# Where the first norm's token rows are loaded and who makes the convolution's small copies, in a decoder layer on one NeuronCore

## The chip, the core and the metric

The kernel runs on one core of one Trainium2 chip. A core has five engines that work side by side, each on its own list of instructions, in order: TensorE (PE in the profile; its weight loads are shown apart as PEld), VectorE (DVE), ScalarE (ACT), GpSimd (POOL) and SyncE (SP), which here issues the DMA transfers. They wait for each other by semaphores. The metric is device time in microseconds (us) of one execution. Lower is better.

## What is computed

One decoder layer over 2048 tokens of 1024 channels, in float32: a norm, one input projection whose columns feed two token mixers (an S5 state space group and an RG-LRU group), an output projection with residual, a second norm with a SwiGLU network, and a last norm. The part that matters here:

```python
h = rms_norm(x, norm1_g[l])
proj = h @ w_in[l]
u = proj[..., :W_S5]
xr = proj[..., W_S5:W_S5 + W_LRU]
yr = proj[..., W_S5 + W_LRU:]
...
xpad = jnp.pad(xf, ((0, 0), (CONV_WIDTH - 1, 0), (0, 0)))
conv = conv_b.astype(f32) + sum(xpad[:, k:k + seq, :] * cw[k] for k in range(CONV_WIDTH))
```

and `rms_norm` multiplies each token's row by 1/sqrt(mean(x^2) + eps) and a gain for each channel.

## The kernel before

The tokens are cut into four blocks of 512 (TB). Data is held with channels on the 128 partitions and the tokens of a block along the free dimension, so the input projection of a block is twelve products, each of 8 chunks of 128 input channels. A float32 operand is split into a high and a low part, and each chunk takes three matmuls (high by high, high by low, low by high): 24 matmuls for one product. Each weight unit is loaded in two parts of 256 KB (`wraw`), cast to its high part on ACT (`whi`), and its low part is a subtraction on DVE or POOL (`wlo`); block 0 stores the low parts for the other blocks (`wlc`).

The norm's factor is not applied to x. The products are made from x times the gain, and each product's result is multiplied by the factor of its token on its way out of PSUM (`rs`, 128 x 512, the same row on all partitions). That is done by `evac_u`, `conv` and `gate_y`. The factor comes from a second copy of the same tokens with the tokens on the partitions (`xn`, four loads of 128 tokens x 1024 channels, 512 KB each): `stat_load` loads one, `stat` squares it on ACT and adds up its columns in the same instruction, `rsqrt` makes the inverse root on DVE in thirteen small steps, and `SumSq.spread` spreads it by TensorE to all partitions and copies it out on ACT. Until `rs` is there, no product leaves PSUM. The products have two banks `acc`, and the third and fourth product of block 0 go to two further ones, `y`.

The convolution (`conv`, four times in a block) puts a product, times the factor, into `xr` behind the last four columns of the block before, which are kept in `halo`; L660 on ACT makes the first tap, three instructions L663 on DVE the others.

Meanwhile the S5 tables are built once, by long runs of small instructions on DVE and POOL (`s5_build`, `s5_table`, `s5_w`, `s5_cp`). `s5_build` is held back on DVE until the first norm's inverse root has been made (`tc.issue_after(last["rs"])`, L560).

The order is a plan: `at(t, fn)` puts a piece of work at a time t of a written schedule (in units of its own, negative ones for what precedes the first product), the pieces are run through in order of t, and a scheduler then orders each engine's list by that priority and by when it reckons that operands are ready. The finished lists are fixed. Tiles come from pools: a tile of one tag with `bufs=1` is filled again only when its last reader is done. `xq` is such a tile; `rT` with `bufs=2` in the code of the change is two tags, `r` and `T`, with two tiles each of 128 x 2 x 512, first used by the gates of block 0 (L675) and by `decay`.

SP issues nearly all transfers, in order. In the plan the first ones are the first half of the first weights (-18.0), x in four loads of 512 KB (-17.9, -17.0, -15.0, -14.9), the second half (-15.4), the first token rows (-13.0), then the following weights (from -12.8), the other token rows behind (-10.5, -8.0, -5.5), and `eye` at -1.0, which `SumSq.spread` needs.

Of the kernel before, what the change touches and what calls it, by code (L numbers as in the profile page):

```python
# [13 lines left out]
ALU = mybir.AluOpType  # L14
# [3 lines left out]
SEQ, DM, TB = 2048, 1024, 512  # L18
# [4 lines left out]
CT = 8  # L23
NC = SEQ // CT
CB = TB // CT
# [34 lines left out]
class Plan:  # L60
# [3 lines left out]
    def at(self, t, fn):  # L64
        self.ev.append((t, len(self.ev), fn))
# [14 lines left out]
def build(tc, nc, I, O, ctx):  # L80
    pl = Plan()
    at = pl.at
    PE, DV, AC, GP, SP = nc.tensor, nc.vector, nc.scalar, nc.gpsimd, nc.sync
# [6 lines left out]
    eye = P.tile([128, 128], F32, name="eye")  # L90
    sA, sQ = ExitStack(), ExitStack()
    A = sA.enter_context(tc.tile_pool(name="A", bufs=1, side="right", reuse_waits="tile"))
    Q = sQ.enter_context(tc.tile_pool(name="Q", bufs=1, reuse_waits="tile"))
# [20 lines left out]
    halo = P.tile([128, 4, 4], F32, name="halo")  # L114
    h0 = P.tile([128, 4], F32, name="h0")
# [18 lines left out]
    xT, out = I["xT"], O  # L134

    def pc(name, i=None, n=1):
        if name in MCOLS:
            a, b = MCOLS[name]
            return pmat[:, a:b]
        a, b = PCOLS[name]  # L140
        return par[:, a:b] if i is None else par[:, a + i:a + i + n]
# [6 lines left out]
    def act(**kw):  # L148

        ins = AC.activation(**kw)  # L150
        ins = getattr(ins, "ins", ins)
        if "i" in last:
            tc.add_manual_dep(ins, last["i"].name, NOSYNC, reason="tables")
        last["i"] = ins

    def aux(tag, bufs=1):
        return PS.tile([128, TB], F32, tag=tag, name=tag, bufs=bufs)
# [7 lines left out]
    def r_(ap):  # L165
        return ap.bitcast(R)
# [54 lines left out]
    def rsqrt(ss, n, room):  # L221

        w_ = ss.shape[-1]
        mp, y, b = (room[:, (i + 1) * w_:(i + 2) * w_] for i in range(3))
        v = P.tile([128, 3, w_], F32, tag=f"nv{w_}", name="nv", bufs=2)
        ms, w, r = v[:, 0, :], v[:, 1, :], v[:, 2, :]
        DV.tensor_scalar(out=mp, in0=ss, scalar1=1.0 / n, scalar2=EPS, op0=ALU.mult, op1=ALU.add)

        DV.tensor_scalar(out=b.bitcast(I32), in0=mp.bitcast(I32), scalar1=1, scalar2=None, op0=ALU.logical_shift_right)
        DV.tensor_copy(out=ms, in_=mp)  # L230
        DV.tensor_scalar(out=y.bitcast(I32), in0=b.bitcast(I32), scalar1=-1.0, scalar2=float(0x5F3759DF),
                         op0=ALU.mult, op1=ALU.add)
        for i in range(3):
            DV.scalar_tensor_tensor(out=w, in0=y, scalar=-0.5, in1=ms, op0=ALU.mult, op1=ALU.mult)
            DV.tensor_tensor(out=w, in0=w, in1=y, op=ALU.mult)
            ins = DV.scalar_tensor_tensor(out=r if i == 2 else y, in0=w, scalar=1.5, in1=y, op0=ALU.add, op1=ALU.mult)
        last.setdefault("rs", getattr(ins, "ins", ins))
        return r
# [69 lines left out]
    pL = sL.enter_context(tc.tile_pool(name="L", bufs=1, reuse_waits="tile"))  # L308
    pW = sW.enter_context(tc.tile_pool(name="W", bufs=1, side="right", reuse_waits="tile"))
    pmat = pW.tile([128, NMAT], F32, name="pmat")  # L310
    at(-1.0, lambda: SP.dma_start(eye, I["eye"]))
    at(4.0, lambda: SP.dma_start(pmat, I["pmat"]))


# [25 lines left out]
    def s5_build():  # L340
        def sm(name, shape=(128, NQ, 16)):
            return pW.tile(list(shape), F32, name=name)
# [5 lines left out]
        em, h, x2, kk, p = (sm(n) for n in ("em", "h", "x2", "kk", "p"))  # L348
# [40 lines left out]
        nr, ni, s, a, c, cr, ci = (sm(n, (128, NQ)) for n in ("nr", "ni", "ss", "aa", "cc", "cr", "ci"))  # L389
# [25 lines left out]
        Q, Qd = (t.rearrange("p a b -> p (a b)").rearrange("p (r q j) -> p r q j", r=2, q=NQ) for t in (mag, em))  # L415
# [5 lines left out]
        TT(out=tq, in0=Pi[:, :, 0:8], in1=crb, op=ALU.mult)  # L421
        TT(out=Q[:, 1], in0=Q[:, 1], in1=tq, op=ALU.add)
        for t in range(CT):
            DV.tensor_copy(out=Qd[:, :, :, t], in_=Q[:, :, :, CT - 1 - t])

        N = [cm[:, :, 0:CT + 1], h[:, :, 0:CT + 1]]
        TS(out=N[0], in0=Pr[:, :, 0:CT + 1], scalar1=-1.0, scalar2=None, op0=ALU.mult)
# [131 lines left out]
    def s5_start():  # L559
        with tc.issue_after(last["rs"]):  # L560
            s5_build()
# [23 lines left out]
    def lt(tag, shape=(128, 2, TB), dt=F32, bufs=1):  # L585
        return pL.tile(list(shape), dt, tag=tag, name=tag, bufs=bufs)
# [19 lines left out]
    def nat(ap):  # L606
        return ap.rearrange("p (t c) -> p c t", t=CT)

    def seq(ap):
        return ap.rearrange("p (c t) -> p c t", t=CT)  # L610

    def in_tb(b, t0):
        H, L = actH, actL
        cur = {}
        sl = SumSq(4, "sumg", 2)
        tx, dx = (t0 - 6.5, 0.5) if b == 0 else (t0 - 5.0, 0.6)
        ts = t0 - 4.0 if b == 0 else t0 - 58.0
# [11 lines left out]


        def stat_load(i):
            cur["q", i] = lt("xq", (128, DM), bufs=1)
            SP.dma_start(cur["q", i], I["xn"][b * TB + 128 * i:b * TB + 128 * i + 128, :])

        def stat(i):
            if i == 0:
                cur["ss"] = P.tile([128, 4], F32, tag="ssq", name="ssq", bufs=2)
            q = cur.pop(("q", i))
            AC.activation(out=q, in_=q, func=AF.Square, accum_out=cur["ss"][:, i:i + 1])

        for i in range(4):
            at(ts + 2.5 * i - (9.0 if b == 0 else 5.0), lambda i=i: stat_load(i))
            at(ts + 2.5 * i, lambda i=i: stat(i))
        at(ts + 9.0, lambda: cur.__setitem__("rs", SumSq.spread(rsqrt(cur["ss"], DM, aux("nm")))))

        def evac_u(m):
            us = v_us[:, m % 2, :]
# [5 lines left out]
        def conv(m):  # L653
            h, i = divmod(m, 2)
            xr, xh = v_xr[i], v_xh[h]
            DV.tensor_copy(out=xr[:, 0:4], in_=halo[:, m, :])
            DV.tensor_tensor(out=seq(xr[:, 4:TB + 4]), in0=nat(cur.pop(("ps", 4 + m))), in1=nat(cur["rs"]),
                             op=ALU.mult)
            DV.tensor_copy(out=halo[:, m, :], in_=xr[:, TB:TB + 4])
            AC.activation(out=xh[:, i, :], in_=xr[:, 4:TB + 4], func=AF.Identity,  # L660
                          bias=pc("cb", m), scale=pc("cw", 12 + m))
            for k in (2, 1, 0):
                DV.scalar_tensor_tensor(out=xh[:, i, :], in0=xr[:, 1 + k:1 + k + TB],  # L663
                                        scalar=pc("cw", 4 * k + m), in1=xh[:, i, :],
                                        op0=ALU.mult, op1=ALU.add)
            if i == 1:
                AC.copy(r_(v_hh), xh)
                GP.tensor_tensor(out=r_(v_hl), in0=xh, in1=v_hh, op=ALU.subtract)
# [23 lines left out]
        def scan():  # L692
            for h in range(2):
                a, q = cur["r", h], cur["T", h]

                DV.scalar_tensor_tensor(out=a, in0=a, scalar=1.0, in1=q, op0=ALU.add, op1=ALU.mult)
                AC.activation(out=a, in_=a, func=AF.Identity, scale=-1.0, bias=1.0)
                act(out=q, in_=q, func=AF.Sqrt)
                DV.scalar_tensor_tensor(out=q, in0=a, scalar=1.0, in1=q, op0=ALU.add, op1=ALU.mult)
                DV.tensor_tensor(out=q, in0=q, in1=v_xh[h], op=ALU.mult)  # L700
                for i in range(2):
                    m = 2 * h + i
                    DV.tensor_tensor_scan(out=q[:, i, :], data0=a[:, i, :], data1=q[:, i, :],
                                          initial=h0[:, m:m + 1], op0=ALU.mult, op1=ALU.add)
                    DV.tensor_copy(out=h0[:, m:m + 1], in_=q[:, i, TB - 1:TB])

        def gate_y(m):
            h, i = divmod(m, 2)
# [18 lines left out]
        t = t0  # L727
        for i, m in enumerate((4, 5, 6, 7, 0, 1, 2, 3, 8, 9, 10, 11)):
            u = Unit(t, I["w_in"][m], 8, GP if i % 3 == 2 else DV, *((wlc[m], None) if b == 0 else (None, wlc[m])))

            def prod(m=m, u=u, i=i):
                cur["ps", m] = aux("y", 2) if b == 0 and i in (2, 3) else acc()
                mm3(cur["ps", m], u, [(k, k) for k in range(8)], chunks_of(H), chunks_of(L), True, True)

            at(t, prod)
            t += 8 * PT
            if m < 4:
                at(t + 0.5, lambda m=m: evac_u(m))
            elif m < 8:
                at(t + 0.5, lambda m=m: conv(m - 4))  # L740
            else:
                at(t + 0.5, lambda m=m: gate_y(m - 8))
            if i == 3:
                at(t + 0.2, lambda: gates(0))
                t += 2.6
            if i == 5:
                at(t + 0.2, lambda: gates(1))
                t += 2.6
                at(t + 2, decay)
                at(t + 2 + 3, scan)  # L750
            if i in (9, 11):
                at(t + 1.0, lambda h=i // 11: lru_out(h))
# [4 lines left out]
    for b in range(NB):  # L757
        tin.append(T)
        T = in_tb(b, T)
# [800 lines left out]
```

## Time and profile before

| what | us |
|---|---|
| three runs, median (lowest to highest) | 2141.07 (2137.44 to 2143.06) |
| the profiled execution's own time | 2144.24 |
| its span, first to last instruction | 2142.5 |
| input projection, S5 tables and LRU of all blocks, about | 0 to 460 |

How to read the lines that follow. A line of the timeline has the start, the time taken, the engine, the line of the kernel, the operation, what it writes and reads, the count, and in brackets how long the engine had been idle and what ended that. A line of the groups has the count, busy time in all, mean in ns of one, and the idle time in front of the group with what ended it. A line of the waits says who waited for whom: us in all, times, longest. SPq is SP's list of transfers; its durations are those of issuing one, not of the transfer. A table by stage has the stretch, its length, busy time and count for each engine, the clock granted to TensorE, the DMA engines' share and their rate.

### The profile page before, as it was taken

The numbers are of one execution on the slowest core, as the hardware profiler recorded it, in microseconds if no ns is written. First come the engines' busy times: TensorE is split into PE (matmuls) and PEld (weight loads), VectorE is DVE, ScalarE is ACT, GpSimd is POOL, SyncE is SP. The second block draws the span as 40 slices with busy tenths as digits, with TensorE's granted clock in tenths as the row PEclk, the third lists the DMA queues.
The fourth block names the chain that finished last, engine by engine and source line by source line (L and its number), as shares of the span: only waits on it lengthen the run. The fifth ranks groups of instructions, "written<-read, shape, count | busy, mean of one in ns | idle before, by whom it ended". The sixth has DMA issues, their size and how long they took to land.

```text
span 2142.5 us, 26006 instructions
## 1 busy us (share of the span) xinstructions
PE 1949.6 (91%) x8600; PEld 1556.4 (73%) x8600; DVE 1220.4 (57%) x1927; ACT 797.4 (37%) x1308; POOL 1012.7 (47%) x836
## 2 busy tenths in 40 slices
PE   6849999887989987999999989999999999999996
PEld 4637777765767766777777767777777888888785
DVE  5997578478547676544444554444434436654644
ACT  4634654463253242223223442322322343333331
POOL 1576246458734458655455543123123237544542
PEclk8968999988999989999999999999999999999998
DMA  8656998875644788644444564444443578754733
GB/s 292 203 171 194 270 298 260 225 191 158 201 128 144 245 273 298 213 149 156 148 146 159 192 206 148 127 139 147 126 140 124 186 257 306 268 186 137 228 102 103
DMA packets 262118, 409.41 MB, mean 191 GB/s; under 512 B 60480, under 2 KB 82272, under 8 KB 261984
## 3 DMA queue, kind: packets, MB, share of 16 engines
q1 hardware_dynamic: 261984, 407.76, 60.5%
q8 instruction: 67, 1.10, 0.2%
q14 instruction: 67, 0.55, 0.1%
HBM read 282.60 MB, written 125.06 MB: 190 GB/s over the span
## 4 chain that ended last, share of the span: by engine, by line
PE 63%; DVE 14%; DMA 10%; issue 4%; POOL 3%; ACT 3%; SPq 2%; POOLq 0%; DVEq 0%; ACTq 0%
PE acc L1215 9%; PE y L1215 9%; PE gt L1215 9%; PE acc L214 5%; PE v L1215 5%; PE nm L1215 5%; PE y L1355 4%; PE acc L1355 4%; PE gt L1355 4%; PE nm L1355 2%; PE v L1355 2%; PE gt L214 2%; DMA wraw<-w_in 1%; DMA wlo<-wlc 1%; DMA hx<-r2d 1%
## 5 line engine op out<-in xcount | busy, mean ns | idle before, releaser
L1228 POOL TENSOR_TENSOR t<-t 128x512 f32<-128x512 f32 x66 | 101.0, 1530 | 346.0 <-DVE t L1254 219.4
L1055 ACT CAST whi<-ws 128x512 fp32r<-128x512 f32 x176 | 109.2, 621 | 338.9 <-PE y L1215 90.2
L214 PE MATMUL acc<-actH,whi 128*128 128x512 f32 x416 | 172.9, 418 | 36.7 <-DVE gy L712 14.1
L214 PE MATMUL acc<-actL,whi 128*128 128x512 f32 x416 | 172.8, 416 | 22.4 <-DVE actL L296 19.6
L1056 DVE TENSOR_TENSOR wlo<-ht,whi 128x512 fp32r<-128x512 f32 x112 | 107.4, 960 | 125.8 <-ACT whi L1055 122.6
L214 PE MATMUL acc<-actH,wlo 128*128 128x512 f32 x416 | 170.6, 411 | 1.3 <-DMA wlo<-wlc 1.1
L1055 ACT CAST whi<-ht 128x512 fp32r<-128x512 f32 x154 | 95.1, 619 | 167.5 <-PE nm L1355 69.2
L1056 DVE TENSOR_TENSOR wlo<-wraw,whi 128x512 fp32r<-128x512 f32 x88 | 75.8, 861 | 138.6 <-ACT whi L1055 138.5
L1056 DVE TENSOR_TENSOR wlo<-ws,whi 128x512 fp32r<-128x512 f32 x176 | 134.3, 763 | 34.4 <-ACT whi L1055 34.3
L1215 PE MATMUL y<-xh,whi 128*128 128x512 f32 x308 | 123.7, 401 | 11.8 <-ACT t L1247 9.9
L1056 POOL TENSOR_TENSOR wlo<-ht,whi 128x512 fp32r<-128x512 f32 x42 | 58.8, 1400 | 157.0 <-ACT whi L1055 155.0
L1215 PE MATMUL acc<-xh,wlo 128*128 128x512 f32 x308 | 122.3, 397 | 7.4 <-DVE wlo L1056 7.4
L214 PEld LDWEIGHTS acc<-actH,whi 128*128 128x128 f32 x416 | 82.9, 199 | 60.3 <-issue 21.0
L1215 PE MATMUL y<-xh,wlo 128*128 128x512 f32 x308 | 122.3, 397 | 2.0 <-DVE wlo L1056 2.0
L1215 PE MATMUL gt<-xh,wlo 128*128 128x512 f32 x308 | 121.4, 394 | 1.3 <-DVE wlo L1056 1.3
L1215 PE MATMUL y<-xl,whi 128*128 128x512 f32 x308 | 122.1, 396 | 0.0
L1215 PE MATMUL acc<-xh,whi 128*128 128x512 f32 x308 | 121.9, 396 | 0.0
L1215 PE MATMUL acc<-xl,whi 128*128 128x512 f32 x308 | 121.7, 395 | 0.0
L1215 PE MATMUL gt<-xh,whi 128*128 128x512 f32 x308 | 121.4, 394 | 0.0
L1215 PE MATMUL gt<-xl,whi 128*128 128x512 f32 x308 | 121.3, 394 | 0.0
L214 PEld LDWEIGHTS acc<-actL,whi 128*128 128x128 f32 x416 | 83.0, 200 | 47.8 <-DVE actL L296 27.9
L1055 ACT CAST whi<-wraw 128x512 fp32r<-128x512 f32 x88 | 54.6, 621 | 150.6 <-PE y L1215 53.0
(459 smaller groups left out, 5442.6 us busy)
## 6 DMA issues: line engine op xcount, KB each, us to landing
td<-t SPq DMA_DIRECT2D x154, 256.0 KB, 2.2
ht<-td SPq DMA_DIRECT2D x154, 256.0 KB, 3.2
wraw<-w_down SPq DMA_DIRECT2D x99, 256.0 KB, 4.4
wraw<-w_in SPq DMA_DIRECT2D x96, 256.0 KB, 5.3
scd<-ws SPq DMA_DIRECT2D x88, 256.0 KB, 2.1
ws<-scd SPq DMA_DIRECT2D x88, 256.0 KB, 2.6
wlo<-wlc SPq DMA_DIRECT2D x72, 256.0 KB, 4.9
xc<-xT SPq DMA_DIRECT2D x56, 256.0 KB, 4.8
```

Source lines behind the costliest of these rows:

```text
L214: PE.matmul(ps, lhsT=part[w][:, kw % 4, :], rhs=r_(x(kx)), start=first and i == 0 and j == 0, stop=last and i == n - 1 and j == 2)
L1055: AC.copy(hi, raw)
L1056: eng.tensor_tensor(out=lo, in0=raw, in1=hi.bitcast(F32), op=ALU.subtract)
L1215: PE.matmul(ps, lhsT=a[:, k, :], rhs=x, start=j in FIRST and k == 0 and i == 0, stop=k == 3 and i == 2, skip_group_check=True)
L1228: (DV if q == 0 else GP).tensor_tensor(out=g, in0=c, in1=g, op=ALU.mult)
L1355: PE.matmul(BK[p][i], lhsT=a[:, i, :], rhs=x, start=j in FIRST and s == 0 and v == 0, stop=s == NSL - 1 and v == 2, skip_group_check=True)
```

## The change

Three things are changed.

1. In block 0 the four loads of token rows go to the four tiles `r`, `r`, `T`, `T`, which nobody uses yet, so that none waits for the square of the one before. All four are planned right behind the last load of x (-14.8 to -14.5), with `eye` behind them (-14.3), and so ahead of all weights but the first product's. Their squares are planned 0.5 apart, the inverse root at `ts + 2.5` and not `ts + 9.0`. Blocks 1 to 3 keep `xq` and their times.
2. In `conv` the last four columns are no longer copied out of `xr`: they are formed a second time from the product in PSUM and the factor, by a DVE product of 128 x 4. (In the product the tokens are ordered by their place in a group of eight first, so the last four are the last column of four rows.) The copy of the old `halo` into `xr` goes to ACT.
3. Two further sets of small DVE copies go to ACT: the eight that reverse `Q` into `Qd` (128 x 32 each), and the one that keeps the last column of the scan (`h0`, 128 x 1, sixteen times).

```diff
-    at(-1.0, lambda: SP.dma_start(eye, I["eye"]))
+    at(-14.3, lambda: SP.dma_start(eye, I["eye"]))
...
         for t in range(CT):
-            DV.tensor_copy(out=Qd[:, :, :, t], in_=Q[:, :, :, CT - 1 - t])
+            AC.copy(Qd[:, :, :, t], Q[:, :, :, CT - 1 - t])
...
         def stat_load(i):
-            cur["q", i] = lt("xq", (128, DM), bufs=1)
+            if b == 0:
+                cur["q", i] = lt("rT"[i // 2], bufs=2).rearrange("p i t -> p (i t)")
+            else:
+                cur["q", i] = lt("xq", (128, DM), bufs=1)
             SP.dma_start(cur["q", i], I["xn"][b * TB + 128 * i:b * TB + 128 * i + 128, :])
...
         for i in range(4):
-            at(ts + 2.5 * i - (9.0 if b == 0 else 5.0), lambda i=i: stat_load(i))
-            at(ts + 2.5 * i, lambda i=i: stat(i))
-        at(ts + 9.0, lambda: cur.__setitem__("rs", SumSq.spread(rsqrt(cur["ss"], DM, aux("nm")))))
+            at(-14.8 + 0.1 * i if b == 0 else ts + 2.5 * i - 5.0, lambda i=i: stat_load(i))
+            at(ts + (0.5 if b == 0 else 2.5) * i, lambda i=i: stat(i))
+        at(ts + (2.5 if b == 0 else 9.0), lambda: cur.__setitem__("rs", SumSq.spread(rsqrt(cur["ss"], DM, aux("nm")))))
...
             xr, xh = v_xr[i], v_xh[h]
-            DV.tensor_copy(out=xr[:, 0:4], in_=halo[:, m, :])
-            DV.tensor_tensor(out=seq(xr[:, 4:TB + 4]), in0=nat(cur.pop(("ps", 4 + m))), in1=nat(cur["rs"]),
-                             op=ALU.mult)
-            DV.tensor_copy(out=halo[:, m, :], in_=xr[:, TB:TB + 4])
+            ps, rs = cur.pop(("ps", 4 + m)), cur["rs"]
+            AC.copy(xr[:, 0:4], halo[:, m, :])
+            DV.tensor_tensor(out=seq(xr[:, 4:TB + 4]), in0=nat(ps), in1=nat(rs), op=ALU.mult)
+
+            end = [v.rearrange("p (t c) -> p t c", t=CT)[:, CT - 4:CT, CB - 1] for v in (ps, rs)]
+            DV.tensor_tensor(out=halo[:, m, :], in0=end[0], in1=end[1], op=ALU.mult)
...
-                    DV.tensor_copy(out=h0[:, m:m + 1], in_=q[:, i, TB - 1:TB])
+                    AC.copy(h0[:, m:m + 1], q[:, i, TB - 1:TB])
```

## The prediction

> **What bounds the kernel now.** I read the profile in this order: busy time per engine and the chain of work that ended last (the page), a table of busy times by stage, then the timeline of the first 50 us. The page shows a TensorE-bound kernel.
>
> ```profile
> span 2142.5 us, 26006 instructions
> PE 1949.6 (91%) x8600; PEld 1556.4 (73%) x8600; DVE 1220.4 (57%) x1927; ACT 797.4 (37%) x1308; POOL 1012.7 (47%) x836
> PE 63%; DVE 14%; DMA 10%; issue 4%; POOL 3%; ACT 3%; SPq 2%; POOLq 0%; DVEq 0%; ACTq 0%
> ```
>
> That is the average; the change lies in the first 460 us, where it is otherwise. The stages (stretch, its length, busy us of PE, weight load, DVE, ACT, POOL with counts, granted clock, DMA share, GB/s):
>
> ```profile
> 0.00:18.73 18.73, 11.16 (x35) 8.64 (x36) 13.85 (x56) 11.22 (x18) 3.09 (x7) 1.00 0.87 307
> 18.73:42.15 23.42, 14.08 (x63) 11.32 (x61) 6.01 (x16) 8.37 (x14) 3.15 (x3) 0.91 0.97 366
> 42.15:53.50 11.35, 7.05 (x24) 5.79 (x25) 8.94 (x57) 4.24 (x7) 0.00 (x0) 0.59 0.36 116
> 53.50:165.66 112.16, 71.60 (x259) 53.09 (x257) 111.78 (x181) 53.75 (x82) 71.56 (x70) 0.80 0.60 182
> 165.66:214.00 48.34, 44.37 (x220) 35.64 (x221) 36.41 (x65) 23.57 (x37) 33.17 (x27) 0.91 0.68 205
> 214.00:321.00 107.00, 99.47 (x520) 78.17 (x519) 68.68 (x124) 63.17 (x94) 38.13 (x42) 0.98 1.03 283
> 321.00:454.00 133.00, 113.96 (x569) 90.56 (x567) 86.17 (x158) 65.54 (x99) 64.11 (x85) 0.92 0.88 239
> ```
>
> From 53.50 to 165.66 VectorE (DVE) is busy 111.78 of 112.16 us while TensorE stands still for 40.6: DVE binds there. Just before, from 18.73 to 42.15, DVE works 6.01 of 23.42 us: 17.4 idle, and 2.4 more up to 53.50. From 165.66 on TensorE is busy 92%, 93% and 86%. So the question is how much of the 19.8 us of idle DVE time the change fills. The timeline says what ends it:
>
> ```profile
> 13.58 1.06 ACT L639 ACTIVATE xq<-xq 128x1024 f32<-128x1024 f32 x1
> 24.51 1.06 ACT L639 ACTIVATE xq<-xq 128x1024 f32<-128x1024 f32 x1 [1.69 <-DMA xq<-xn]
> 32.03 1.06 ACT L639 ACTIVATE xq<-xq 128x1024 f32<-128x1024 f32 x1 [0.61 <-DMA xq<-xn]
> 40.97 1.06 ACT L639 ACTIVATE xq<-xq 128x1024 f32<-128x1024 f32 x1 [6.91 <-DMA xq<-xn]
> 42.15 0.17 DVE L227 TENSOR_SCALAR nm<-ssq 128x4 f32<-128x4 f32 x1 [11.03 <-ACT xq L639]
> 44.52 0.16 DVE L236 SCALAR_TENSOR_TENSOR nv<-nv,nm 128x4 f32<-128x4 f32 x1
> ...
> 32.42 0.39 PE L214 MATMUL y<-actH,wlo 128*128 128x512 f32 x1
> 44.73 2.07 PE L275 MATMUL nm<-eye,nv 128*128 128x128 f32 x8 [11.92 <-DVE nv L236]
> 48.52 0.80 PE L214 MATMUL acc<-actH,whi 128*128 128x512 f32 x1 [1.72 <-DVE xr L657]
> ```
>
> The four squares of the first norm (L639) run one by one, each after a load into the only xq buffer; the last ends at 42.1. Then the inverse root runs (42.15 to 44.68), is spread over PSUM, and frees the banks: TensorE, which had filled its four banks at 32.81, goes on at 48.52. The building of the S5 tables is tied behind that root (L560), so DVE's long queue starts there too.
>
> **The change, part by part.** *The loads.*
>
> ```profile
> 5.53 1.68 SPq L182 DMA_DIRECT2D wraw<-w_in  x3
> ...
> 12.30 0.33 SPq L311 DMA_DIRECT2D eye<-eye  x1
> 13.57 0.33 SPq L312 DMA_DIRECT2D pmat<-pmat  x1
> ...
> SPq L311 <- DMA y<-xT: 1.0, 1, 1.0
> SPq L312 <- DMA xq<-xn: 0.9, 1, 0.9
> ...
> 14.64 1.65 ACT L188 CAST whi<-wraw 128x512 fp32r<-128x512 f32 x3
> 16.33 0.39 PE L214 MATMUL acc<-actH,whi 128*128 128x512 f32 x1
> ```
>
> The eye issue waited until y landed (12.30), the pmat issue until the first token rows landed (13.57): one 512 KB load takes 1.27 us when it follows another. Three more stand now at that place, ahead of all further weights: they land near 14.8, 16.1 and 17.4, and eye (64 KB, an eighth) takes 0.16. SP issues four DMAs more there, some 0.5 us each (three weight issues took 1.68), within the time in which earlier loads are still landing. The squares, 1.2 us each with the read of the accumulator (40.97 to 42.15), end at 18.6 instead of 42.1. The price: the weights behind land 3.97 us later. The second product's three casts ran from 14.64; now the first can begin at about 18.6, behind the last square, and the product at 19.2 instead of 16.33: **2.9 us** of wait for TensorE, and 35.7 instead of 32.81 for the fourth product. What that wait covers today is nothing, but it lies in a stage that gets 15.7 us (32.81 to 48.52) back: with the first bank freed before 35.7, TensorE goes on at once, 12.8 us earlier.
>
> *What DVE gets.* The root starts at 18.6 and takes 2.5 us, more if lo-splits (0.69 each) and POOL come between; the factor is spread (2.07 on TensorE) and copied, so it stands at 24 to 27. From 21 DVE has the S5 build, which needs no TensorE. At most it fills all 19.8 us. It loses some: the convolutions of products two to four now wait for their products (before, the first four had all been done by 32.81), in an order fixed beforehand, and the root's chain has steps that wait for one another. I take 5 for this (0 to 9, the latter the 2.9 of TensorE twice and 3 for a root held by POOL), leaving **14.8**.
>
> *The small copies.*
>
> ```profile
> L659 DVE COPY halo<-xr 128x4 f32<-128x4 f32 x16 | 7.3, 468 | 0.0
> L656 DVE COPY xr<-halo 128x4 f32<-128x4 f32 x16 | 4.8, 318 | 0.0
> L424 DVE COPY em<-mag 128x32 f32<-128x32 f32 x8 | 4.8, 670 | 0.0
> L705 DVE COPY h<-T 128x1 f32<-128x1 f32 x16 | 1.7, 140 | 0.0
> L424 DVE COPY em<-mag x8: 183/297/1542, 102.9 to 106.4; 128x32 f32<-128x32 f32 x8
> ...
> 57.87 3.47 POOL L668 TENSOR_TENSOR hl<-xh,hh 128x1024 fp32r<-128x1024 f32 x1 [22.47 <-ACT hh L667]
> 58.97 2.40 DVE L656 COPY xr<-halo 128x4 f32<-128x4 f32 x1
> 107.61 1.30 DVE L530 TENSOR_TENSOR tmp<-tab,se 128x8 f32<-128x8 f32 x1
> 109.04 0.29 DVE L533 TENSOR_TENSOR tab<-tab,tmp 128x8 f32<-128x8 f32 x1
> 142.49 2.62 DVE L445 TENSOR_TENSOR tw<-pmat,em 128x1024 f32<-128x1024 f32 x1
> 191.01 0.15 DVE L227 TENSOR_SCALAR nm<-nm 128x4 f32<-128x4 f32 x1
> L271 ACT COPY row<-nm 4x128 f32<-4x128 f32 x3 | 0.7, 249 | 2.4 <-PE nm L269 2.4
> ```
>
> Before 165.66, where DVE binds, lie all of L424 (4.8), the 2.40 of one L656, and little else: 8 us at face value. Much of that is waiting: the 2.40 copy ends at 61.37, POOL's 3.47 at 61.34, and the other fifteen copies of L656 take 0.18 each (16 x 0.318 less 2.40). A 128x8 product took 1.30 in one place and 0.29 in another, so the next instruction on DVE may inherit the wait. Without waits L424 is 8 x 0.183 = 1.5, the others 0.5: the gain is 2 to 8, less the four new halo products out of PSUM (0.15 each, as L227 on four PSUM columns; 0.3 at worst): **net 1 to 7, I take 3**, nearer the low end because of the product that waited too. ScalarE gets 40 copies of 0.2 to 0.25: 8 to 10 us over 450, hidden while it is busy 53.75 of 112.16.
>
> The Trainium skill, "SBUF — State Buffer", section Who interferes with whom, says that a VectorE copy in its two-port mode, or one with two SBUF inputs, and a GpSimd instruction shut each other out for a whole instruction, and that one with a single SBUF input does not take part. The rows agree (2.40 ending with POOL's 3.47). By that rule the wait passes to the next two-input instruction and the copies give 1, the total 2127.5; by the durations they give 7, the total 2122.3.
>
> *Waits added.* The new halo product waits for ACT to have read the old halo; behind it on DVE stand three L663 and the next lo-split, for which ACT (L667) and TensorE wait, and it holds the PSUM bank of its product until it is done. The xr copy on ACT waits for the L663 of two convolutions earlier; behind it stand L660 and the weight casts. The Qd copies wait for L422 and are next needed by W at 142.49 (L445), 35 us after the last of them. The h0 copy waits for the scan; the next scan of that row is a block later. I cost these at nothing, on ACT's slack; uncovered they are the third rival.
>
> *The sum.* 14.8 + 3 = 17.8 us at 165.66 (12 to 27). Behind that TensorE leads, and shifted starts pass on, except where it idles for others: 8%, 7% and 14% of the three stretches. I take the largest off: 17.8 x 0.86 = **15.3**. The later halo and h0 copies (about 8 us) lie beside a busier TensorE: 0 to 3, I take 0. The profiled execution took 2144.24 (span 2142.5 and 1.7 around it): 2128.9. The median of the runs is 3.17 below it: **2125.8**.
>
> **The rivals.**
> 1. *Everything comes back*: all 19.8 idle us filled and the copies' waits gone, 27 at 165.66, plus 3 later: 2111. For it: POOL stands idle for 22.47 us before 57.87, so DVE work moved into that time meets no POOL instruction. Against: DVE must wait for products two to four.
> 2. *The DMA stretch takes half.* From 214 to 321 the DMA share is 1.03; if its transfers and not TensorE set the pace, an earlier start only waits there. For it: that share. Against: TensorE is busy 93% in it, and the stretch before has a DMA share of 0.68, room for transfers to start earlier. Half of 15.3: 2133.4.
> 3. *Slower: DVE becomes the hostage of ACT.*
>
> ```profile
> L639 ACT ACTIVATE xq<-xq 128x1024 f32<-128x1024 f32 x16 | 16.9, 1058 | 28.8 <-DMA xq<-xn 28.8
> L663 DVE SCALAR_TENSOR_TENSOR xh<-xr,par,xh 128x512 f32<-128x512 f32 x48 | 40.9, 867 | 6.5 <-ACT xh L660 6.2
> ```
>
> If the halo copy on ACT stands behind a square that waits for its load (28.8 us in 12 waits, 2.4 each), all 16 convolutions stop DVE and hold a bank for it: 38.4, less 15.3: 2164. It cancels the gain from 0.96 us for each convolution, and is slower by 0.3% from 1.36. For it: ACT works in order. Against: DVE already waits for ACT's L660 in each convolution, only 6.2 in all, and the copy needs nothing new.
> 4. *It does not do what it says*: the root is still placed late in DVE's or TensorE's order, and the squares being early helps nobody: only the copies, 2139 to 2141.
>
> **How the numbers follow.** A measurement of this kernel can tell about 0.3% (6.4 us) from no change, so faster means below 2134.6. Forecast (gain 10 to 21, 2120 to 2131): 0.48. Rival 1 (2111 to 2119): 0.12. Rival 2 (2132 to 2139): 0.20, half of it counted as faster. Rival 3: 0.12. Rival 4: 0.06, no change. The 0.02 left is split. Faster 0.48 + 0.12 + 0.10 = 0.70, same 0.10 + 0.06 + 0.01 = 0.17, slower 0.13. The range 2111 to 2139 holds the forecast and rivals 1 and 2: 0.80.
>
> **What would show it.** Four squares back to back from about 13.6 to 18.6; a TensorE gap of about 3 us near 16; the fifth product near 36; DVE without its 11.03 gap and the first convolution of block 1 (165.66 now) near 148. L424 gone from DVE with the following products longer says that the wait was inherited. Wrong would be: a gap on DVE in front of the halo products longer than 1 us (rival 3), the factor's spread later than 35 (rival 4), or 148 reached but lost again by 321 (rival 2).

## The result and the profile after

| kernel | us, median (lowest to highest) |
|---|---|
| before, four runs beside the changed one | 2139.26 |
| changed, four runs | 2121.24 (2120.48 to 2127.57) |
| ratio changed to before, 95% interval | 0.9926, 0.9905 to 0.9946 |
| profiled execution of the changed kernel | 2121.99, span 2120.1 |

The change is faster by 18.0 us of the medians. The forecast was a gain of 15.3, to 2125.8; the time lies 4.6 us below it and inside the range.

The page of the changed kernel, its span and busy times and the shares of the chain of work that ended last:

```profile
span 2120.1 us, 26001 instructions
...
PE 1949.6 (92%) x8600; PEld 1560.2 (74%) x8600; DVE 1211.6 (57%) x1887; ACT 803.6 (38%) x1348; POOL 1030.7 (49%) x836
...
PE 63%; DVE 11%; DMA 11%; POOL 6%; issue 4%; ACT 4%; SPq 1%; POOLq 0%; DVEq 0%; ACTq 0%
```

TensorE is busy as long as before, 1949.6 us: what went is time in which it stood still. In the chain DVE's share fell from 14% to 11% and POOL's rose from 3% to 6%; what that says of the copies is asked below.

The timeline of the changed kernel, at the steps that the prediction named (start, time taken, engine, line, what is written and read, and in brackets the idle time in front):

```profile
13.03 1.06 ACT L642 ACTIVATE r<-r 128x1024 f32<-128x1024 f32 x1
...
16.90 1.06 ACT L642 ACTIVATE T<-T 128x1024 f32<-128x1024 f32 x1 [0.17 <-DMA T<-xn]
18.08 0.17 DVE L227 TENSOR_SCALAR nm<-ssq 128x4 f32<-128x4 f32 x1 [1.22 <-ACT T L642]
18.61 0.79 PE L214 MATMUL acc<-actH,whi 128*128 128x512 f32 x1 [3.48 <-ACT whi L188]
27.10 0.59 ACT L278 COPY rs<-nm 128x512 f32<-128x512 f32 x1 [0.50 <-PE nm L275]
28.12 1.08 DVE L661 TENSOR_TENSOR xr<-acc,rs 128x512 f32<-128x512 f32 x1
37.37 0.39 PE L214 MATMUL acc<-actH,whi 128*128 128x512 f32 x1
53.21 0.77 PE L214 MATMUL acc<-actH,whi 128*128 128x512 f32 x1 [3.37 <-DVE us L651]
144.80 1.05 DVE L661 TENSOR_TENSOR xr<-acc,rs 128x512 f32<-128x512 f32 x1
```

The four squares (the first and the last are shown) stand back to back, 1.3 us apart, and the root starts at 18.08 instead of 42.15. TensorE pays 3.48 us in front of the second product (18.61), and then runs without a stop past its fifth product (37.37 instead of 48.52) up to 49.84 (53.21 less its 3.37 of idle time). The first convolution of block 1, the mark by which the prediction measured, comes at 144.80 instead of 165.66: 20.9 us earlier.

One row by stage of the changed kernel (length, busy us and count of PE, weight load, DVE, ACT and POOL, granted clock, DMA share, GB/s):

```profile
18.08:53.50 35.42, 31.52 (x135) 25.81 (x136) 34.84 (x100) 17.11 (x30) 9.89 (x5) 0.94 0.88 318
```

Behind the mark the two kernels have to be compared over the same work, not over the same times. The first convolution of block 2 starts at 236.22 instead of 257.73, that of block 3 at 335.66 instead of 359.66: the lead of 20.9 us is 21.5 and 24.0 there. From the mark to block 3, first before, then changed:

```profile
165.66:359.70 194.04, 178.77 (x927) 141.33 (x928) 134.02 (x241) 103.82 (x158) 95.77 (x98) 0.97 0.89 255
```

```profile
144.80:335.70 190.90, 174.83 (x916) 139.26 (x916) 131.39 (x231) 108.68 (x179) 99.38 (x101) 0.97 0.90 267
```

TensorE stands 15.3 us in the first and 16.1 in the second, at the same granted clock, so the lead passes on whole. (Some of its growth is another order of the work: 916 matmuls lie in the stretch instead of 927.)

The next rows go from the first to the 55th matmul that reads `aH` and `whi` and writes `acc`. Every kernel timed here does the same 898 matmuls in between (those at the edges can add one or two to the count of a row). Before, then changed:

```profile
424.09:646.42 222.33, 186.90 (x898) 146.36 (x899) 143.94 (x253) 101.91 (x161) 137.13 (x165) 0.92 0.61 169
```

```profile
395.03:625.95 230.92, 188.97 (x899) 149.39 (x898) 142.08 (x247) 101.39 (x162) 146.23 (x165) 0.89 0.58 164
```

For this the changed kernel takes 8.6 us longer: TensorE stands 6.5 us more and is busy 2.1 us longer for the same matmuls, at a granted clock of 0.89 instead of 0.92. Its lead is 29.1 us at the start of the stretch (some of that is another order of the work) and 20.5 at the end.

### The profile page after: what moved, and what is told of

The parts are those of the page before. It is cut to its first block, busy times and chain, and to the rows that moved or that the text cites. A ratio compares the mean times of both kernels' runs of the same rounds, so it can differ in the third digit from the quotient of the medians.

```text
span 2120.1 us, 26001 instructions
## 1 busy us (share of the span) xinstructions
PE 1949.6 (92%) x8600; PEld 1560.2 (74%) x8600; DVE 1211.6 (57%) x1887; ACT 803.6 (38%) x1348; POOL 1030.7 (49%) x836
## 4 chain that ended last, share of the span: by engine, by line
PE 63%; DVE 11%; DMA 11%; POOL 6%; issue 4%; ACT 4%; SPq 1%; POOLq 0%; DVEq 0%; ACTq 0%
PE acc L1220 9%; PE gt L1220 9%; PE y L1220 9%; PE acc L214 5%; PE v L1220 5%; PE nm L1220 5%; PE y L1360 4%; PE acc L1360 4%; PE gt L1360 4%; PE nm L1360 2%; PE v L1360 2%; DMA wraw<-w_in 2%; PE gt L214 1%; DMA ht<-xcd 1%; DMA hx<-r2d 1%
```

## The experiments

Each kernel was timed beside the kernel before, on the same chip; e1 to e4, e5 to e8 and e9 to e12 are three such groups, and the changed kernel itself stands in a fourth, above, so that between groups the ratios are to be compared. A ratio is not exactly that of two medians. The last column but one is the start of the first convolution of block 1 (165.7 before, 144.8 in the changed kernel), from each kernel's timeline.

| run | what it is | us, median | ratio, 95% interval | mark | root |
|---|---|---|---|---|---|
| e1 | loads alone | 2116.08 | 0.9893, 0.9877 to 0.9909 | 144.8 | 17.8 |
| e2 | copies alone | 2131.61 | 0.9976, 0.9960 to 0.9993 | 151.9 | 41.1 |
| e3 | changed, second product's weights first | 2111.20 | 0.9875, 0.9854 to 0.9895 | 145.2 | 19.0 |
| e4 | idle tiles alone, planned times as before | 2115.68 | 0.9896, 0.9877 to 0.9915 | 143.1 | 21.2 |
| e5 | changed, `h0` copies back on DVE | 2118.07 | 0.9905, 0.9881 to 0.9928 | 146.0 | 18.4 |
| e6 | changed, `Qd` copies back on DVE | 2116.07 | 0.9902, 0.9869 to 0.9935 | 147.2 | 17.9 |
| e7 | changed, convolution's copies as before | 2121.58 | 0.9922, 0.9899 to 0.9944 | 145.0 | 17.8 |
| e8 | e3 without any of the copies' moves | 2114.90 | 0.9892, 0.9872 to 0.9913 | 148.7 | 20.1 |
| e9 | before, S5 tables not tied to the root | 2133.45 | 0.9977, 0.9962 to 0.9992 | 170.4 | 61.3 |
| e10 | changed, 6 us more work on DVE | 2116.27 | 0.9899, 0.9884 to 0.9915 | 144.9 | 18.6 |
| e11 | e3 again, five runs | 2112.99 | 0.9893, 0.9875 to 0.9912 | 146.0 | 20.0 |
| e12 | e3 with the tables not tied | 2117.54 | 0.9902, 0.9886 to 0.9919 | 150.7 | 23.4 |

### Loads alone, copies alone

e1 keeps `h0`, `Qd` and the convolution's copies on DVE as they were; e2 keeps the loads as they were and moves the copies. The edits are the two halves of the diff above:

```diff
 e1, against the kernel before
-    at(-1.0, lambda: SP.dma_start(eye, I["eye"]))
+    at(-14.3, lambda: SP.dma_start(eye, I["eye"]))
-            cur["q", i] = lt("xq", (128, DM), bufs=1)
+            if b == 0:
+                cur["q", i] = lt("rT"[i // 2], bufs=2).rearrange("p i t -> p (i t)")
...
-            at(ts + 2.5 * i - (9.0 if b == 0 else 5.0), lambda i=i: stat_load(i))
+            at(-14.8 + 0.1 * i if b == 0 else ts + 2.5 * i - 5.0, lambda i=i: stat_load(i))
...
 e2, against the kernel before
-            DV.tensor_copy(out=Qd[:, :, :, t], in_=Q[:, :, :, CT - 1 - t])
+            AC.copy(Qd[:, :, :, t], Q[:, :, :, CT - 1 - t])
...
-                    DV.tensor_copy(out=h0[:, m:m + 1], in_=q[:, i, TB - 1:TB])
+                    AC.copy(h0[:, m:m + 1], q[:, i, TB - 1:TB])
```

> The kernel before with the first part of the change alone (token rows of block 0 into the r and T tiles behind x, eye behind them, squares and root planned earlier); all small copies stay on VectorE. Theory A (VectorE's idle time before 53.5 us was the loss, the early root fills it): 12 to 17 us faster than the kernel before, first convolution of block 1 near 148 to 151, after 165.7 before and 144.8 with the whole change. Rival B (the small copies with their waits for GpSimd are the larger part of the 18 us): no more than 6 us faster, first convolution of block 1 not before 155.

> The kernel before with the second and third part alone (halo out of PSUM, small copies on ScalarE); loads as before. Theory A: 1 to 6 us faster than the kernel before, the fifth product still near 48, first convolution of block 1 at 159 to 165. Rival B: 10 us or more faster.

The loads alone give all of it: the mark at 144.8, where the whole change has it too, and a time that is no longer than the whole change's (2116.08 against 2121.24, with intervals that overlap by 0.0004). Theory A of e1 came out, with both sizes too small: it expected 148 to 151 at the mark and 12 to 17 us in the total, and 144.8 and 23.0 (between the medians) were measured. The copies alone give 13.8 us at the mark (151.9, where 159 to 165 was expected), with the root still at 41.1; but at the first convolution of block 2 (250.03 instead of 257.73) 7.7 us are left, and in the total 0.24% (5 us; 7.5 between the medians). So the two parts don't add: 20.9 and 13.8 together make 20.9.

The tables from the root to the mark: first the whole change, then the loads alone, then the copies alone:

```profile
18.08:144.80 126.72, 94.22 (x353) 73.00 (x353) 125.10 (x231) 64.41 (x112) 88.45 (x74) 0.84 0.69 226
```

```profile
17.80:144.80 127.00, 92.23 (x353) 72.51 (x353) 124.13 (x246) 63.49 (x98) 77.89 (x74) 0.83 0.71 233
```

```profile
41.10:151.90 110.80, 78.36 (x281) 59.95 (x281) 107.47 (x222) 59.24 (x105) 72.41 (x63) 0.79 0.61 193
```

With the copies gone from it, DVE has 15 instructions fewer before the mark (231 against 246) and is busy just as long (125.10 against 124.13), and POOL, with the same 74 instructions, is busy 10.6 us longer (88.45 against 77.89). That fits two engines that each wait inside the other's instructions (two POOL products shown further below are an example). The chains of waits say where the path went. The kernel before, up to its mark (start, time, engine and line; the pieces in between are left out):

```profile
101.65 1.26 DVE mag L422
102.94 4.75 DVE em L424 x8
107.69 1.22 DVE tmp L530
...
165.74 0.94 DVE xr L657
```

The changed kernel:

```profile
96.86 1.81 POOL wlo L189
...
100.12 1.47 POOL tcp L445
...
110.55 2.22 POOL tcp L445
112.77 1.57 POOL tab L529
114.34 1.57 POOL tab L531
115.90 1.58 POOL tmp L530
```

The copies alone:

```profile
101.82 1.29 ACT em L424 x8
...
108.60 6.43 POOL wlo L189
115.03 1.97 POOL CP L447
...
144.31 2.47 POOL gy L721
```

Before, the path from L422 on is DVE, the 4.75 us of L424 among it. In the changed kernel and with the copies alone it runs over POOL and its half of the S5 tables instead: from 96.86 to 117.48, and from 108.60 to 146.78. It is tempting to call that a new bound which moving the copies put in the place of DVE, but two other runs speak against it. e4 (see the next section) leaves every copy on DVE, and its path runs over POOL all the same:

```profile
103.96 2.23 POOL wlo L189
...
132.71 1.48 POOL gy L722
```

e10 has every copy moved, and its path from 90 to 124.9 is DVE's. In e1, at the same mark, the chain stays on DVE up to 124.6 and ends on a product of TensorE:

```profile
122.63 1.94 DVE actL L296
124.61 4.82 PE acc L214 x13
...
138.38 6.36 PE acc L214 x20
144.76 2.06 DVE xr L660 x2
```

So up to the mark several paths are about equally long, and which of them ends last changes with the order of the lists. The releasers are inferred. Where the 13.8 us of the copies alone come from stays open: that kernel reaches L422 no earlier than the one before (101.5 and 101.7), so they all arise behind it, and no run splits them.

### What in the loads does it

e4 takes the kernel before and gives block 0's token rows the four idle tiles, and nothing else: their loads stay at their planned times, behind the weights.

```diff
-            cur["q", i] = lt("xq", (128, DM), bufs=1)
+            if b == 0:
+                cur["q", i] = lt("rT"[i // 2], bufs=2).rearrange("p i t -> p (i t)")
+            else:
+                cur["q", i] = lt("xq", (128, DM), bufs=1)
```

> The kernel before with the idle tiles alone: block 0's token rows go to the r and T tiles, planned times of loads, squares and root as before, so that each load has one weight part between it and the next. Theory A: the waiting for the one buffer was what made the root late, not the planned place; the last square ends near 20 and the kernel is 10 to 16 us faster than before. Rival D (the place right behind x and the earlier planned root are needed, as the fixed order otherwise puts the root late): last square early, but root or its spread after 30, less than 6 us faster.

In the timeline of e4 the root starts with

```profile
21.20 0.17 DVE L227 TENSOR_SCALAR nm<-ssq 128x4 f32<-128x4 f32 x1 [2.79 <-ACT T L642]
```

3.1 us later than in the changed kernel, and the mark (143.1) comes no later and the total (2115.68) is no longer than with the loads alone. The total gained more than the expected 10 to 16 us (23.4 between the medians). So the single buffer held the norm back: each load waited for the square before it. The place of the loads in SP's list and the new planned times are worth nothing that these runs show.

e3 and e8 put the loads of the second product's two weight parts ahead of three of the four token loads, with (e3) and without (e8) the copies' moves. Against the changed kernel, and e8 against e1:

```diff
-    at(-14.3, lambda: SP.dma_start(eye, I["eye"]))
+    at(-9.8, lambda: SP.dma_start(eye, I["eye"]))
...
-            at(-14.8 + 0.1 * i if b == 0 else ts + 2.5 * i - 5.0, lambda i=i: stat_load(i))
+            at((-14.8, -10.1, -10.0, -9.9)[i] if b == 0 else ts + 2.5 * i - 5.0, lambda i=i: stat_load(i))
```

> The changed kernel, with the second to fourth load of token rows and eye put behind the two weight parts of the second product. Both theories: TensorE's gap of 3.48 us at 18.61 shrinks below 0.7, the last square ends some 1.3 us later than 18.08. Theory A (VectorE binds up to block 1): no gain from that, total within 3 us of the changed kernel (2118 to 2124), first convolution of block 1 at 144 to 147. Rival C (TensorE's gap is paid in full): 3 us or more faster than the changed kernel, 2118 or less, and the lead shown at the first convolution of block 1 too.

> The loads alone (all small copies on VectorE) with the token rows two to four behind the second product's weights. If both gains (5 us without the copies, 10 us with the weights first) are of their own kind they add: 2104 to 2108. If both only shuffle the order behind block 1 (theory F), it lies like the others, 2108 to 2117. TensorE's gap near 18 below 0.7 us in both.

TensorE's 3.48 us in front of the second product are gone (0.3 us is its longest wait there in e8), for a root that is 0.9 to 2.0 us later. But TensorE stops a little later instead, in e3 for the low parts of later weights:

```profile
31.87 0.50 PE L214 MATMUL y<-actH,wlo 128*128 128x512 f32 x1 [1.58 <-DVE wlo L189]
35.42 0.50 PE L214 MATMUL acc<-actH,whi 128*128 128x512 f32 x1 [0.49 <-ACT whi L188]
40.02 0.79 PE L214 MATMUL acc<-actH,wlo 128*128 128x512 f32 x1 [3.87 <-DVE wlo L189]
```

Up to 60 us it stands 5.9 us in e3 and 6.9 in the changed kernel (3.48 and the 3.37 at 53.21). So the gap was moved more than removed, and the mark does not move for it (145.2) or comes later (148.7), as theory A of e3 had it. The total of e3, though, went the way of rival C: 2111.20, 10 us below the changed kernel and the lowest of all; a gain that the mark does not show is not explained by the gap. e8 lies with its second case: the two gains don't add. Since e3 was the lowest, it was run again:

> The best version again, in five rounds. If it truly beats the changed kernel, its ratio to before lies between 0.985 and 0.990 and the interval ends below 0.9915; if the earlier 0.9875 was the lucky end of the scatter that all versions with early loads share, it comes out at 0.990 to 0.993.

2112.99 and 0.9893 in five runs. Its two sets of runs, four and five, thus have medians of 2111 and 2113, against 2121 for the changed kernel. The upper end, 0.9912, is still above the changed kernel's lower end, 0.9905, and the loads alone have 0.9893 as well. It beats the kernel before by 1.1 to 1.2%, and very probably the changed kernel; that it beats the loads alone is not shown.

### The copies, one set at a time

Each of e5, e6 and e7 takes the changed kernel and puts one set back on DVE:

```diff
 e5
-                    AC.copy(h0[:, m:m + 1], q[:, i, TB - 1:TB])
+                    DV.tensor_copy(out=h0[:, m:m + 1], in_=q[:, i, TB - 1:TB])
 e6
-            AC.copy(Qd[:, :, :, t], Q[:, :, :, CT - 1 - t])
+            DV.tensor_copy(out=Qd[:, :, :, t], in_=Q[:, :, :, CT - 1 - t])
 e7
-            AC.copy(xr[:, 0:4], halo[:, m, :])
+            DV.tensor_copy(out=xr[:, 0:4], in_=halo[:, m, :])
...
-            DV.tensor_tensor(out=halo[:, m, :], in0=end[0], in1=end[1], op=ALU.mult)
+            DV.tensor_copy(out=halo[:, m, :], in_=xr[:, TB:TB + 4])
```

> The changed kernel with the sixteen h0 copies back on VectorE. Without the small copies the kernel was 5 us faster than the whole change (2116.1 against 2121.2), though both had block 1's first convolution at 144.8. Theory E (ScalarE stands behind the scan for its h0 copy, 26.5 us in 13 waits, and its casts and the half clock after TensorE's gaps pay for it): 4 to 7 us faster than the changed kernel, 2114 to 2117, and TensorE's busy time at half clock down from 102.7 towards 85. Theory F (no single copy does it; each variant gets another fixed order, and the gaps of TensorE fall otherwise): within 3 us of the changed kernel or off by a few us to either side, like the two other returns.

> The changed kernel with the eight Qd copies back on VectorE. By the sum of the prediction they give a part of 3 us at block 1's first convolution: it moves from 144.8 to 146 to 149, the total by 0 to 3 us more than the changed kernel's. Theory E: no faster than the changed kernel. Theory F: anything from 2114 to 2126, with no bond to what the convolution's mark shows.

> The changed kernel with the convolution as before (halo copied out of xr, both small copies on VectorE); loads, Qd and h0 changed. Theory E: as slow as the changed kernel, 2119 to 2124, since the h0 copies stay on ScalarE. A rival G (the halo copy on ScalarE, 11.1 us of waits, and the bank held longer by the halo product are what costs): 2114 to 2117. Theory F: anything from 2114 to 2126.

2118.07, 2116.07 and 2121.58, with intervals that all hold 0.991: theory F of e5, that no single copy does it, is not contradicted. No set is a gain on top of the loads, and none is shown to be a loss. Putting `Qd` back, the set that the prediction gave its price, moves the mark by 2.4 us (147.2), within what was expected, but the total, expected 0 to 3 us longer than the changed kernel's, is 5 shorter. What the moves cost ACT is in its groups in the first 460 us of the changed kernel, with the first two rows for DVE:

```profile
L668 DVE SCALAR_TENSOR_TENSOR xh<-xr,par,xh 128x512 f32<-128x512 f32 x48 | 45.1, 949 | 4.5 <-ACT xh L665 4.2
L664 DVE TENSOR_TENSOR halo<-acc,rs 128x4 f32<-128x4 f32 x14 | 2.2, 156 | 0.0
...
L710 ACT COPY h<-T 128x1 f32<-128x1 f32 x16 | 3.0, 191 | 26.5 <-DVE T L708 26.5
L660 ACT COPY xr<-halo 128x4 f32<-128x4 f32 x16 | 3.0, 190 | 11.1 <-DVE xh L668 7.7 <-DVE nv L234 2.4 <-DVE nm L231 1.0
```

ACT stands 26.5 us for the scans and 11.1 for the copies into `xr`, with all that is queued behind. But the halo products on DVE never wait (0.0), and DVE waits for the first tap no longer than before (4.2 us against 6.2). ACT's slack covers it.

### Is it VectorE's idle time?

The prediction's price was idle DVE time that gets filled. e9 fills it in another way: the kernel before, without the tie that holds the S5 tables behind the root. e10 asks it from the other side: the changed kernel with more to do on DVE, 15 products of 128 x 256 at the head of the S5 build, whose result is written over.

```diff
 e9, against the kernel before
-        with tc.issue_after(last["rs"]):
-            s5_build()
+        s5_build()
 e10, against the changed kernel
+        for _ in range(15):
+            TT(out=p, in0=mul_b, in1=mul_b, op=ALU.mult)
```

> The kernel before with one line less: the building of the S5 tables is no longer tied behind the inverse root; loads and copies are as before, so the root still starts at about 42. Theory (idle VectorE time is the loss): VectorE works in 18 to 42 all the same, the first convolution of block 1 comes at least 10 us earlier (155 or earlier instead of 165.7), and the total falls by 8 to 15 us, though TensorE still stands from about 33 to 48. Rival (TensorE's stand before the fifth product is the loss): the fifth product still starts at 48 to 50, and the total falls by less than 4.

> The kernel after with 15 products of 128x256 more on VectorE at the head of the S5 build (their result is overwritten; about 0.34 us each, 5.1 in all). Theory (VectorE binds up to the first convolution of block 1): the mark goes from 144.8 to 149 to 151, and the total rises by 3 to 6 us against after. Rival (something else binds there since the change): the mark moves by less than 2 and the total by less than 2.

e9 fell outside both expectations. Stages, root and spread of e9 (the stages and the steps are two views):

```profile
18.73:42.15 23.42, 14.14 (x63) 11.37 (x61) 23.15 (x77) 7.58 (x13) 7.38 (x9) 0.85 0.98 347
42.15:82.80 40.65, 2.07 (x8) 1.78 (x8) 38.28 (x77) 5.19 (x9) 36.15 (x49) 0.50 0.29 95
```

```profile
61.31 0.15 DVE L227 TENSOR_SCALAR nm<-ssq 128x4 f32<-128x4 f32 x1
77.47 2.07 PE L275 MATMUL nm<-eye,nv 128*128 128x128 f32 x8 [44.59 <-DVE nv L236]
83.89 0.80 PE L214 MATMUL acc<-actH,whi 128*128 128x512 f32 x1 [0.46 <-DVE xr L656]
```

DVE's idle time is filled as in the changed kernel (23.15 us busy of 23.42, against 6.01). But the long build now stands in front of the root, which slips from 42.15 to 61.31, its steps lie among the build's and take until 77.25, and TensorE, with full banks, stands for 44.59 us. The mark comes 4.7 us later than before, and still the total is 0.23% lower. So DVE work done early does not bring the mark forward by itself when the root comes late for it. e9 mixes the two and can't price either.

e10's extra products took

```profile
L356 DVE TENSOR_TENSOR p<-par x15: 407/417/421, 22.8 to 42.3; 128x256 f32<-128x256 f32 x15
```

15 x 0.417 = 6.3 us on DVE ahead of the mark, and cost nothing: the mark is at 144.9, the total at 2116.27. From the root to the mark e10 has this row, to be held against the changed kernel's 125.10 and 88.45:

```profile
18.55:144.90 126.35, 92.96 (x352) 71.56 (x353) 125.48 (x244) 65.59 (x114) 79.71 (x72) 0.84 0.71 235
```

DVE is busy as long with 6.3 us more work in it, and POOL 8.7 us less with two instructions fewer. So the idea that the sum of DVE's work sets the mark in the changed kernel falls. "Busy" there must hold some 6 us or more of waiting, which more work displaces. The rival's side of the expectation held at the mark: something else binds, in the changed kernel's chain POOL's tables, in e10's two loads and a product of TensorE at the end. The total, expected within 2 us of the changed kernel's, is 5.0 lower. More work can't be the reason for that; like every edit, the extra products gave the lists another order.

e12 is e3 with the tie taken away:

> The best version with the S5 tables no longer tied behind the inverse root. With early loads the root runs at 19.0, so theory: VectorE has at most the stretch between its first work and 21 left to win, 2 to 3 us at the first mark of block 1 (145.2 to about 143) and 0 to 3 in the total. Rival: the build now runs ahead of the root and its factor, which come later by several us; the fifth product waits and the total is 2 to 5 us longer than the best version.

The rival held: root at 23.4 instead of 20.0, mark at 150.7 instead of 146.0, the total 4.6 us longer than e11's (with intervals that overlap). With an early norm the tie shows no cost and keeps the root in front.

## Why the prediction was right, and where not

**The loads.** Squares to 18.6 (the root could start at 18.08), a wait of 2.9 us in front of the second product (3.48), the fifth product near 36 (37.37), the factor at 24 to 27 (its copy ran from 27.10 to 27.69): each step came as worked out or just behind. e4 shows the cause that the prediction named, the one buffer.

**What DVE gets.** "I take 5 for this" was wrong. From 18.08 to 53.50 DVE is busy 34.84 of 35.42 us; from 18.73 to 53.50 it had been 6.01 + 8.94 of 34.77. By these rows all 19.8 us were filled and none lost: the S5 build, free from 21.5 on, had enough small work for each wait of the root and of the convolutions. As busy time can hold waiting, the mark says it better: the loads alone bring 20.9 us there, where the forecast had 14.8 for them. That is also more than the 19.8 which the prediction took for the most that can be filled, so filled idle time is not quite the whole account.

**The small copies.** The step "net 1 to 7, I take 3" failed in its form: there is no one price. Alone, the copies brought 13.8 us at the mark (and 5 in the total); on top of the loads, none. The working took DVE as the only bound and added. The chains show DVE, POOL's tables, or loads and TensorE ending last in one run or another, at marks within a few us of each other; so once the loads have relieved DVE, the copies find nothing to win. Forecast 14.8 + 3 = 17.8 at the mark; measured 20.9 + 0. The sum was near because its two errors were of opposite sign, and in the totals that is plainer still: the loads, priced at 14.8 x 0.86 = 12.7 us, brought 23.0 by themselves, and the whole change 18.0 where 15.3 was forecast. That the total came out so near is luck.

The prediction drew on the Trainium skill, "SBUF — State Buffer", section Who interferes with whom, and worked out from its rule that a wait passes to the next two-input instruction. The rows fit that for the copies on top of the loads: 15 instructions fewer and the same busy time. In POOL's timeline of the changed kernel two equal products of the tables lie side by side, the first in a gap of DVE's two-input work and the second not:

```profile
102.38 0.41 POOL L531 TENSOR_TENSOR tab<-tab,se 128x128 f32<-128x128 f32 x1
102.75 1.40 POOL L530 TENSOR_TENSOR tmp<-tab,se 128x128 f32<-128x128 f32 x1
```

Yet the copies alone moved the mark by 13.8, more than their 8 us of face value, so the rule tells who waits for whom and not what the sum becomes.

**Passing on.** "17.8 x 0.86" was the right kind of term for a different course. The lead did not shrink by the idle shares of the three stretches: it was 20.9 us at the mark and 24.0 at the first convolution of block 3, with TensorE standing still as long as before in between (16.1 us and 15.3). It shrank behind, in the 898 matmuls from 395.03 to 625.95, most of which the prediction had not looked at. 18.0 of 20.9 remain in the medians, which happens to be 0.86.

**The rivals.** Rival 1 held for the filling and not for the copies. Rival 2 fell: with a DMA share of 0.90 from the mark to block 3 the lead was not lost. Rival 3 fell: 4.2 us of waits for ACT, none at the halo products. Rival 4 fell: the factor's copy ended at 27.69, not behind 35.

**What stays open.** Between the changed kernel and the loads alone lie 5 us of the medians. In the two profiled executions (spans 2120.1 and 2113.1) the difference arises in the stretch of the same 898 matmuls. The loads alone, then e3:

```profile
397.43:614.27 216.84, 180.46 (x899) 141.78 (x898) 141.23 (x251) 100.56 (x158) 141.65 (x165) 0.93 0.62 174
```

```profile
396.97:615.08 218.11, 181.64 (x900) 142.59 (x898) 141.63 (x247) 101.14 (x162) 140.47 (x165) 0.93 0.61 172
```

The changed kernel took 230.92 us for it, 14.1 more than the loads alone: TensorE is busy 8.5 us longer at a granted clock of 0.89 instead of 0.93, and stands 5.6 us more. (Of the 14.1, 2.4 are given back in front of the stretch and 4.7 behind it.) The moved copies are not shown to be the cause: e3 and e10 have them all moved, and take 218.1 and 218.3 us. That fits theory F of e5, that each variant has another fixed order and the stops of TensorE fall otherwise, but it is argued and not shown. Which stop it is in the changed kernel stays open, and with it whether the copies' moves are worth anything. Not tried were more tiles for the token rows of blocks 1 to 3, which still share `xq` and stand in the changed kernel's chain of waits.

## What to carry to other kernels

Before a resource is moved or enlarged, look for a load that waits for the reader of the one before it: a single buffer in front of a reduction can hold the whole pipeline, and tiles that nobody uses yet are a cheap cure. Don't add the gains of two parts that relieve the same engine: price the second with the first one done, and ask which engine ends last then. Where two engines can wait inside each other's instructions, busy time holds waiting, so a busy share of 99% alone does not show a bound; adding work there and seeing whether the mark moves tells more. And compare two kernels over the same work, between the same instructions: counts in equal stretches of time mix other work in.

## What the runs showed of the hardware

DVE's busy time gave way to 6.3 us of further work without the end moving (125.48 against 125.10 us busy), while POOL's was 8.7 lower. An equal POOL product took 0.41 or 1.40 us.

TensorE's granted clock makes equal work take unequal busy time: the same 898 matmuls were 188.97 us at 0.89 and 180.46 at 0.93. In e9 the clock stood at 0.50 through the 40.65 us in which TensorE had 2.07 us to do. The Trainium skill, "TensorE: Matmul & The Clock Gate", section What's actually happening, says that the clock is halved until the array has been busy for a window of about 3.4 us. The 0.50 of e9 agrees with the halving; how long the window is, these rows don't show. For a kernel with many short stops it would make where the stops fall a cost beside their sum, which no run here takes apart.
